# New TensorE prices in the build-time model that paces the background work of a two-block layer kernel

## The chip, the cores and the metric

The kernel runs on one core of one Trainium2 chip. The metric is device microseconds for one execution of the whole program, as the median of several runs.

## The reference, cut to what matters

256 tokens of width 2048 go through two blocks, one layer each. The first has latent attention beside differential attention, then cross-attention to a memory of 256 tokens, then a gated feed-forward layer of width 5632. The second has an adaptive norm, a wide input projection, a recurrent mix with matrix state (WKV) beside a short convolution, and an output projection. What the change touches most is where one block hands over to the other:

```python
x = x + (silu(hf @ w_gate) * (hf @ w_up)) @ w_down      # end of block 1
x = rms_norm(x, g_final)                                # its last norm
...
h = rms_norm_2(x, pre_gain) * (1.0 + scale) + shift     # block 2
proj = h @ w_in
pa = proj[..., :COLS_A]
pa = pa + (shift_time(pa, 1) - pa) * mu_shift           # token shift: row t takes in row t-1
r, k, v = pa[..., :D_A], pa[..., D_A:2*D_A], pa[..., 2*D_A:3*D_A]
...
S = S * w_t + sa * b_t + v_t * k_t                      # WKV, in chunks in the kernel
```

## The kernel before, in words

Every weight product is done in fp32r in three parts: the weight is split into a high and a low half (`whi`, `wlo`), the activation too, and TensorE (PE) adds `whi` with both halves of the activation and `wlo` with its high half. The weights come from memory in sub-tiles of 512 KB (two k tiles of 128 by 512 columns). For each sub-tile SP issues the load into `raw`, ScalarE (ACT) rounds it to `whi` (`act`, L401), VectorE (DVE) subtracts to get `wlo` (`tt`, L371), and PE runs twelve matmuls (`mm`, L410): eight with `whi`, then four with `wlo`. The rings hold 5 `raw`, 4 `whi` and 4 `wlo` buffers (L345), and `ahead` (L579) writes the splits of the next sub-tiles into the program before the matmuls of the present one. This is the main stream; it is a fixed sequence of sub-tiles over both blocks. The first two sub-tiles of block 2 are staged aside, in `own`.

All else is background work: generators that write a few instructions at each step (norms, transposes `tpose` L414 through the identity, attention, the token shift, the WKV chunks). Those that finish a column block are called posts, the long ones lanes. Nothing on the chip schedules them. The program's order is settled while it is built: after each eight and after each twelve matmuls of the main stream, `poll` (L495) asks a rough model of the engines, `Clock` (L241 to L324), whether a step's inputs will be there, and if so writes the step at that place into the queues of all the engines. The two conditions are that the step is due at least 900 ns before the model's PE time (`EARLY`), and, for lanes, that the modelled DVE and ACT are no more than 3000 ns ahead of PE (`SLACK`):

```python
EARLY, SLACK, ADA_BEAT = -900.0, 3000.0, 2
...
now = ck.t["PE"]
for g in posts + lanes:
    if not g.busy and g.due <= now + g.early and (g in posts or max(ck.t["V"], ck.t["S"]) <= ck.t["PE"] + SLACK):
        step(g)
```

Each engine then runs its own queue strictly in that order and waits where an input is late. So a price in the model moves no instruction from one engine to another; it moves background steps ahead of or behind main-stream instructions in the queues.

Three pieces of background work matter below. `ev_norm` (L1247) does the last norm of block 1 and the norm of block 2 for one half of the tokens, and writes the transposed halves `XA`, from which block 2's first matmuls read. `shift_mix` (L1287) does the token shift of a column block: it zeroes one row, copies the block one partition down by a DMA of GpSimd's (POOL's) queue, and then three DVE operations (subtract, scale, add) use what was copied; `ev_pa` (L1340) calls it for the 384 columns of `k` group 0 and for the 512 columns each of `r` and `v` later. `wkv_lane` (L1416) is the chain of the WKV mix, with `lora` (L1427) and the product with a triangle of ones (`mm` into `bgt`, L1472) at its start.

Of the kernel before, what the change touches and what calls it, by code (L numbers as in the profile page):

```python
# [11 lines left out]
F32R = mybir.dt.float32r  # L12
# [21 lines left out]
# block 2's input projection: the low rank columns lie before the key's  # L34
# [9 lines left out]
COLV = [("g_mix", 16), ("g_xattn", 16), ("g_mem", 16), ("g_ffn", 16), ("pre_gain_2", 16), ("post_gain_2", 16), ("ada_b_2", 48),  # L44
        ("g_q_lat", 4), ("g_kv_lat", 2), ("g_diff_sub", 2)]
# [46 lines left out]
def _kt(n):  # L92
    """k tiles to a transfer of n columns"""
    return 4 if n <= 256 else 2
# [51 lines left out]
class Arena:  # L146
    """Column ranges of one on-chip tile, handed out in program order."""
# [66 lines left out]
class Fixed(Buf):  # L214
    """A part of a tile that is not the arena's."""
# [8 lines left out]
class XT:  # L224
    """A transposed activation, split, 8 k tiles to a part: [128 channels, k, hi/lo, tokens]."""
# [18 lines left out]
class Clock:  # L244
    """A rough model of when each engine reaches what has been issued, to pace the background work."""
# [53 lines left out]
    def pe(self, cols, ins, outs):  # L299
        """the array's clock is halved after a window in which it was mostly idle"""  # L300
        w = int(max(self.t["PE"], self.after(ins, outs, "PE")) / 3413.3)
        self.op("PE", cols / (2.4 if self.cols.get(w - 1, 0) >= 3060 else 1.2) + 3, ins, outs)
        w = int(self.t["PE"] / 3413.3)
        self.cols[w] = self.cols.get(w, 0) + cols
# [18 lines left out]
class Job:  # L323
    """A column block's product: k tiles ka to kb of the weight with the activation's from k0 on.  # L324
    A skewed one runs through the first half of the tokens before the second; half is the
    evacuation of one half then."""
# [9 lines left out]
def kernel(ctx: ExitStack, tc: tile.TileContext, d, out):  # L336
    nc = tc.nc
    V, S, G, PE = nc.vector, nc.scalar, nc.gpsimd, nc.tensor
# [16 lines left out]
    A, A2 = Arena(big, NA - 352), Arena(big, 352, NA - 352)  # L355
# [8 lines left out]
    ck = Clock()  # L364
# [42 lines left out]
    def mm(o, l, r, start=True, stop=True):  # L407
        n = size(o)
        ck.pe(n if l.dtype == F32R else max(4 * n, 512) if l.shape[-1] > 64 else 2.3 * n, [l, r], [o])
        PE.matmul(out=o, lhsT=l, rhs=r, start=start, stop=stop, skip_group_check=True)  # L410

    def tpose(o, i):
        ck.pe(256, [i], [o])
        PE.transpose(o, i, ident)  # L414
# [39 lines left out]
    def rpow(o, a, scale, eps):  # L454
        """o = (a * scale + eps) ** -0.5 for a few columns"""
        ts(o, a, scale, eps, ALU.mult, ALU.add)
        gpow(o)
# [12 lines left out]
    # ------------------------------------------------------------------ engine  # L470
    class Task:
        """A generator, and when what its next step reads is there."""
# [44 lines left out]
    def run(jobs, hook):  # L517
# [6 lines left out]
        def early():  # L524
            """block 2's first weights, staged beside the ring"""
            yield from wait("own_go")
            xc = ck.slot(sb.tile([P, 4, 4, 256], F32R, tag="XC", name="own"), "XC", 1)
            at = [(xc[:, 0], xc[:, 1]), (xc[:, 2], xc[:, 3])]
            for i, (h, l) in zip(sorted(own), at):
                yield from room(1024)  # L530
                raw = buf(4, 256)
                dma(raw.ap, weight(i))
                yield [raw.ap]
                act(h, raw.ap, AF.Copy)
                yield
                tt(l, raw.ap, h.bitcast(F32), ALU.subtract)
                raw.free()
                his[i], los[i] = h, l
# [15 lines left out]
        def pieces(i):  # L554
            """the first one is cut, for an early start"""
            n = subs[i][0].kt
            return [slice(a, a + 1) for a in range(n)] if i == 0 else [slice(0, n)]
# [21 lines left out]
        def ahead(i):  # L579
            """what can be staged while sub-tile i is multiplied"""  # L580
            while True:
                for x in range(3):
                    while at[x] in own:
                        at[x] += 1
                nl, nh, nd = at
                if nl < nh and (nl < i + NL or nl < e0 + 4) and ringed(i, nl) < NL:
                    low(nl)
                    at[0] += 1
                elif nh < nd and (nh < i + NH or nh < e0 + 4) and ringed(i, nh) < NH:
                    high(nh)  # L590
                    at[1] += 1
                elif nd < len(subs) and ringed(nl, nd) < NR:
                    load(nd)
                    at[2] += 1
                else:
                    return
# [49 lines left out]
    # ------------------------------------------------------- transposes, splits  # L646
    def split_t(tr, xt, k, n, gain=None):
        """tr: [128, n, 256] in PSUM, transposed; into xt's k..k+n"""
        if gain is None:
            act(xt.hi(k, n), tr, AF.Copy)  # L650
            tt(xt.lo(k, n), tr, xt.hi(k, n).bitcast(F32), ALU.subtract)
        else:
            for a in range(n):
                hi, lo = xt.hi(k + a), xt.lo(k + a)
                src, gn = tr[:, a:a + 1, :], gain[:, a:a + 1]
                act(hi, src, AF.Copy, scale=gn)
                stt(lo, src, gn, hi.bitcast(F32), ALU.mult, ALU.subtract)
        xt.done(k, n)

    def trans(src, n=2):  # L660
        """natural [128 tokens, 2 halves, n*128] -> PSUM [128, n, 256]"""
        tr = pst("tr", 2).rearrange("p (a t) -> p a t", a=2)
        for a in range(n):
            for th in range(2):
                tpose(tr[:, a, th * P:th * P + P], src[:, th, a * P:a * P + P])
        return tr[:, 0:n, :]
# [8 lines left out]
    def to_t(src, dst, nk):  # L675
        """natural -> transposed fp32 [128, nk, 256]"""
        for a in range(0, nk, 2):
            tr = trans(src[:, :, a * P:(a + 2) * P])
            if a % 4 == 0:
                act(dst[:, a:a + 2, :], tr, AF.Copy)  # L680
            else:
                vcopy(dst[:, a:a + 2, :], tr)
            yield [src]
# [16 lines left out]
    def load_split(src, gain, xt, ahead):  # L700
        """a transposed activation from DRAM, with its gain, split"""
# [28 lines left out]
    # ================================================================ schedule  # L730
    with tc.manual_schedule():
# [28 lines left out]
        # ---- what block 1 keeps  # L760
# [5 lines left out]
        def tables():  # L766
# [32 lines left out]
            # lambda  # L799
# [13 lines left out]
            # tables that carry the norm's factor  # L813
# [17 lines left out]
        def xr_lane():  # L831
            """the residual stream, by column blocks of 512"""
# [8 lines left out]
        # ---- block 1, attention: evacuations  # L841
# [3 lines left out]
        def rope(o, p, cc, ss, n, hd):  # L845
            """o = p * cc + swap(p) * ss for [128, n heads * hd] (p in PSUM)"""
# [54 lines left out]
        def ev_scaled(key, k, nk, r, flag):  # L901
            """scaled by the norm's factor, then transposed"""
# [41 lines left out]
        # ---- attention lanes  # L944
        def softmax_head(score, scale, sums):
            """scores of one head -> exponentials and their sums"""
# [116 lines left out]
        # ---- residual updates  # L1063
        def ev_add(a, n, nxt=None):
            """xr += block; then, if asked for, its squares and its transpose with a gain"""
# [61 lines left out]
        # ---- FFN  # L1127
# [24 lines left out]
        # ---- adaLN vector, in the background of the FFN  # L1152
# [3 lines left out]
        def ada_lane():  # L1156
# [27 lines left out]
            # shift, gain and gate, then as rows  # L1184
# [25 lines left out]
        # ---- end of block 1: final norm, block 2's norm  # L1210
# [36 lines left out]
        def ev_norm(th, p):  # L1247
            """the two norms of a half of the tokens, their factors as one:
            (mean(x^2 g^2) + eps (mean(x^2) + eps)) ** -0.5"""
# [34 lines left out]
        # ================================================================ block 2  # L1284
        b2 = {}

        def shift_mix(raw, col, n):  # L1287
            """token-shift mix of a block [128, 2, n], in place"""
# [13 lines left out]
        def ev_lo(p):  # L1302
            """the low rank part, and the key's first 128 columns"""
# [108 lines left out]
        # ---- WKV  # L1412
# [3 lines left out]
        def wkv_lane(g):  # L1416
# [16 lines left out]
            # normalised key, key and beta  # L1433
# [20 lines left out]
            # decay: chunk factors, cumulated from both ends  # L1454
# [40 lines left out]
            # es: kk^, ep: r^, av: b^, kx: k^  (all natural)  # L1495
# [28 lines left out]
            # stacked operands of the state's update  # L1524
# [8 lines left out]
            # Gram blocks  # L1533
# [12 lines left out]
            # inverses of the 32 x 32 diagonal blocks, one per partition  # L1546
# [64 lines left out]
            # the chain over chunks  # L1611
# [45 lines left out]
            # group norm, bonus, gate  # L1657
# [29 lines left out]
        # ---- merge, output projection, gated residual  # L1687
# [80 lines left out]
        # ================================================================ the jobs  # L1768
# [64 lines left out]
        # ---- background work that starts when a weight is reached  # L1833
        def after(name, w, n=0):
            """a flag that is set when the n-th product with a weight is done"""
# [48 lines left out]
```

## Time and profile before

| | us |
|---|---|
| runs shown | 2036.32, 2033.89, 2034.57 |
| median | 2034.57 |
| profiled execution: span from the first to the last instruction | 2032.9 |
| its own time beside the span | not listed apart; the median lies 1.7 above the span |
| PE busy | 1997.7 |
| DVE busy | 1335.3 |
| ACT busy | 939.6 |
| POOL busy | 192.9 |
| mean granted clock of PE, as a share of full speed | 0.996 |

PE has work for 98% of the span. What it waited for, by engine, line and tile, is listed in the view of waits; the view of windows says in which stretch of the span that was.

### The profile page before, as it was taken

To read this page: it belongs to the slowest core of one execution; us is meant where nothing else is said; L and a number is where in the kernel's file an instruction comes from. 1 tells how busy PE (TensorE), PEld (TensorE's weight loads), DVE (VectorE), ACT (ScalarE), POOL (GpSimd) and SP (SyncE) were. 2 spreads that over 40 slices of the span, in tenths; PEclk is the share of its full clock that TensorE was granted. 3 is DMA by queue.
4 is the path that set the end of the run, shared out by engine and by line. 5 is a ranking of instruction groups with operands and counts; after the bars stand their busy time and mean duration, and the time that the engine had idled before them with its cause. 6 is when DMAs were issued, how large, how long until landed. Compare 5 with 4: busy or idle time off the path is not lost. (4 is left out here: it accounts for less than half of the span.)

```text
span 2032.9 us, 26782 instructions
## 1 busy us (share of the span) xinstructions
PE 1997.7 (98%) x10155; PEld 1663.1 (82%) x10155; DVE 1335.3 (66%) x1672; ACT 939.6 (46%) x1262; POOL 192.9 (9%) x316
## 2 busy tenths in 40 slices
PE   8999999999999999999999988899999999999998
PEld 7877888978888888888888886688888788888887
DVE  6756567456777767777754663768938678936654
ACT  6544458555444344434444453434444544444443
POOL 0000001000010100101000032120121201111000
PEclk9999999999999999999999999999999999999999
DMA  8643647547878888788776645676665666645763
GB/s 297 212 135 117 200 148 251 177 152 272 295 277 284 289 284 281 281 288 307 264 249 191 216 130 161 188 207 197 214 186 178 210 187 187 209 141 183 241 187 124
DMA packets 125056, 436.97 MB, mean 215 GB/s; under 512 B 17142, under 2 KB 17286, under 8 KB 124160
## 3 DMA queue, kind: packets, MB, share of 16 engines
q1 hardware_dynamic: 97776, 348.96, 52.0%
q0 software_dynamic: 26432, 85.19, 13.5%
q8 instruction: 79, 1.29, 0.2%
q10 hardware_dynamic: 720, 1.13, 0.2%
q14 instruction: 49, 0.40, 0.1%
HBM read 420.89 MB, written 5.79 MB: 210 GB/s over the span
## 5 line engine op out<-in xcount | busy, mean ns | idle before, releaser
L371 DVE TENSOR_TENSOR wlo<-raw,whi 128x1024 fp32r<-128x1024 f32 (+3 forms) x661 | 797.3, 1214 | 490.8 <-ACT whi L401 455.8
L401 ACT ACTIVATE whi<-raw 128x1024 fp32r<-128x1024 f32 (+3 forms) x661 | 689.9, 1051 | 627.8 <-PE mm L410 608.6
L410 PE MATMUL mm<-whi,XA 128*128 128x512 f32 (+3 forms) x3776 | 921.3, 385 | 7.3 <-ACT XA L401 5.5
L410 PEld LDWEIGHTS mm<-whi,XA 128*128 128x128 f32 x3776 | 689.3, 189 | 145.7 <-ACT XA L401 5.5
L410 PE MATMUL mm<-wlo,XA 128*128 128x512 f32 (+3 forms) x1888 | 495.0, 385 | 7.4 <-DVE wlo L371 7.4
L410 PEld LDWEIGHTS mm<-wlo,XA 128*128 128x128 f32 x1888 | 345.2, 189 | 77.2 <-DVE wlo L371 8.3
L410 PE MATMUL mm<-whi,XB 128*128 128x512 f32 (+1 forms) x1456 | 324.6, 366 | 0.1
L410 PEld LDWEIGHTS mm<-whi,XB 128*128 128x128 f32 x1456 | 249.9, 189 | 42.4 <-ACT whi L401 0.3
L383 DVE SCALAR_TENSOR_TENSOR arena<-arena 128x1024 f32<-128x1024 f32 (+24 forms) x180 | 180.8, 1005 | 1.5
L410 PE MATMUL mm<-wlo,XB 128*128 128x512 f32 (+1 forms) x728 | 174.3, 365 | 0.0
L410 PEld LDWEIGHTS mm<-wlo,XB 128*128 128x128 f32 x728 | 126.3, 189 | 21.7 <-DVE wlo L371 0.3
L371 DVE TENSOR_TENSOR arena<-arena 128x1024 f32<-128x1024 f32 (+8 forms) x101 | 91.7, 915 | 33.4 <-DMA arena<-arena 25.6
L430 POOL DMA_DIRECT2D arena<-in_ada_w_dram x96 | 50.7, 530 | 472.8 <-DVE arena L383 415.1
L410 PE MATMUL mm<-whi,XC 128*128 128x512 f32 (+1 forms) x368 | 87.3, 377 | 0.0
L401 ACT ACTIVATE arena<-arena 128x512 f32<-128x512 f32 (+5 forms) x84 | 51.3, 615 | 59.2 <-DVE arena L371 33.4
L410 PEld LDWEIGHTS mm<-whi,XC 128*128 128x128 f32 x368 | 64.2, 189 | 11.0
L414 PE MATMUL tr<-cst,arena 128*128 128x128 f32 x402 | 62.6, 274 | 4.6 <-DVE XA L371 3.4
L414 PEld LDWEIGHTS tr<-cst,arena 128*128 128x128 f32 x402 | 49.6, 141 | 17.5 <-DVE XA L371 3.7
L371 DVE TENSOR_TENSOR arena<-arena,mm 128x512 f32<-128x512 f32 (+1 forms) x74 | 44.9, 638 | 17.8 <-PE mm L410 14.4
L426 POOL TENSOR_TENSOR small<-small,cst 128x2 f32<-128x2 f32 (+1 forms) x16 | 11.4, 711 | 473.5 <-DVE small L378 405.8
L410 PE MATMUL bgs<-arena 128*128 128x256 f32 (+3 forms) x200 | 50.3, 360 | 0.0
L401 ACT ACTIVATE arena<-mm,small 128x512 f32<-128x512 f32 (+1 forms) x50 | 30.5, 660 | 35.9 <-PE mm L410 34.1
(126 smaller groups left out, 941.7 us busy)
## 6 DMA issues: line engine op xcount, KB each, us to landing
raw<-in_w_in_dram SPq DMA_DIRECT2D x241, 512.0 KB, 4.2
arena<-in_ada_w_dram POOLq DMA_DIRECT2D x96, 512.0 KB, 5.9
raw<-in_w_gate_dram SPq DMA_DIRECT2D x88, 512.0 KB, 5.0
raw<-in_w_up_dram SPq DMA_DIRECT2D x88, 512.0 KB, 5.0
raw<-in_w_down_dram SPq DMA_DIRECT2D x88, 512.0 KB, 4.6
raw<-in_w_out_dram SPq DMA_DIRECT2D x64, 512.0 KB, 3.6
raw<-in_p_b_dram SPq DMA_DIRECT2D x16, 512.0 KB, 3.5
raw<-in_p_a_dram SPq DMA_DIRECT2D x16, 512.0 KB, 4.5
```

The source lines that it names most:

```text
L371: V.tensor_tensor(out=o, in0=a, in1=b, op=op)
L383: V.scalar_tensor_tensor(out=o, in0=a, scalar=s, in1=b, op0=o0, op1=o1, **kw)
L401: S.activation(out=o, in_=i, func=f, scale=scale, **kw)
L410: PE.matmul(out=o, lhsT=l, rhs=r, start=start, stop=stop, skip_group_check=True)
L414: PE.transpose(o, i, ident)
L426: G.tensor_tensor(out=o, in0=o, in1=nhalf[:, 0:o.shape[1]], op=ALU.pow)
L430: (nc.sync if q == "SP" else nc.gpsimd).dma_start(out=o, in_=i)
```

## The change

The diff takes three prices of the model and replaces them. All its other lines remove comments.

```diff
@@ Clock.pe (L299)
-        self.op("PE", cols / (2.4 if self.cols.get(w - 1, 0) >= 3060 else 1.2) + 3, ins, outs)
+        self.op("PE", cols / (2.4 if self.cols.get(w - 1, 0) >= 3060 else 1.2), ins, outs)
@@ mm (L407)
         n = size(o)
-        ck.pe(n if l.dtype == F32R else max(4 * n, 512) if l.shape[-1] > 64 else 2.3 * n, [l, r], [o])
+        ck.pe(n + 32 if l.dtype == F32R else 4 * n + (224 if n >= 256 else 22), [l, r], [o])
@@ tpose (L412)
-        ck.pe(256, [i], [o])
+        ck.pe(240, [i], [o])
```

No instruction is added or removed: PE has 1105 background matmuls and transposes before and after, DVE 917 instructions of its background, ACT 494, and the order of SP's loads is the same. The places at which background work stands between main-stream instructions differ. Three of them follow, each as it was and as it is now.

PE where block 2 begins and the second half of the tokens is transposed, before (`tr` is a transpose into PSUM, `mm_9440` and `mm_9441` are the sums of the first and the second half of the tokens, `own` one of the two staged sub-tiles):

```order
L410 MATMUL mm_9440<-whi_9386,XA1_9404 128x256 x8
L410 MATMUL mm_9440<-wlo_9388,XA1_9404 128x256 x4
L414 MATMUL tr_9529<-cst_63,arena_66 128x128 x2
L410 MATMUL mm_9441<-own_7381,XA0_9403 128x256 x4
L414 MATMUL tr_9538<-cst_63,arena_66 128x128 x2
L410 MATMUL mm_9441<-own_7381,XA0_9403 128x256 x4
L414 MATMUL tr_9547<-cst_63,arena_66 128x128 x2
L410 MATMUL mm_9441<-own_7381,XA0_9403 128x256 x4
L414 MATMUL tr_9556<-cst_63,arena_66 128x128 x2
```
PE there, after:

```order
L410 MATMUL mm_9440<-whi_9386,XA1_9404 128x256 x8
L414 MATMUL tr_9525<-cst_63,arena_66 128x128 x2
L410 MATMUL mm_9440<-wlo_9388,XA1_9404 128x256 x4
L414 MATMUL tr_9534<-cst_63,arena_66 128x128 x2
L410 MATMUL mm_9441<-own_7381,XA0_9403 128x256 x8
L414 MATMUL tr_9547<-cst_63,arena_66 128x128 x2
L410 MATMUL mm_9441<-own_7381,XA0_9403 128x256 x4
L414 MATMUL tr_9556<-cst_63,arena_66 128x128 x2
```
The first two pairs of transposes stand one group of four matmuls earlier, and the transposes after them have eight matmuls of the second half of the tokens behind them where there were four.

DVE at the token shift of `k` group 0, before (each `wlo` is a sub-tile of the column block `r` group 0; `arena 128x256` and `128x2x128` are steps for the 128 columns that came with the low-rank part, `128x768` those for the 384 columns; the first of each is the one that reads the DMA's copy):

```order
L371 TENSOR_TENSOR wlo_9816<-raw_9711,whi_9814 128x1024
L371 TENSOR_TENSOR wlo_9836<-raw_9730,whi_9834 128x1024
L371 TENSOR_TENSOR arena_66<-arena_66 128x256
L371 TENSOR_TENSOR wlo_9859<-raw_9751,whi_9857 128x1024
L371 TENSOR_TENSOR arena_66<-arena_66 128x256
L371 TENSOR_TENSOR wlo_9878<-raw_9776,whi_9876 128x1024
L371 TENSOR_TENSOR arena_66<-arena_66 128x2x128
L371 TENSOR_TENSOR arena_66<-arena_66 128x768
L371 TENSOR_TENSOR wlo_9898<-raw_9798,whi_9896 128x1024
L371 TENSOR_TENSOR arena_66<-arena_66 128x768
L371 TENSOR_TENSOR wlo_9917<-raw_9818,whi_9915 128x1024
L371 TENSOR_TENSOR arena_66<-arena_66 128x2x384
```
DVE there, after:

```order
L371 TENSOR_TENSOR wlo_9816<-raw_9711,whi_9814 128x1024
L371 TENSOR_TENSOR arena_66<-arena_66 128x256
L371 TENSOR_TENSOR wlo_9837<-raw_9730,whi_9835 128x1024
L371 TENSOR_TENSOR wlo_9859<-raw_9751,whi_9857 128x1024
L371 TENSOR_TENSOR arena_66<-arena_66 128x256
L371 TENSOR_TENSOR arena_66<-arena_66 128x768
L371 TENSOR_TENSOR wlo_9879<-raw_9776,whi_9877 128x1024
L371 TENSOR_TENSOR arena_66<-arena_66 128x2x128
L371 TENSOR_TENSOR arena_66<-arena_66 128x768
L371 TENSOR_TENSOR wlo_9899<-raw_9798,whi_9897 128x1024
L371 TENSOR_TENSOR arena_66<-arena_66 128x2x384
```
The first `128x256` stands one `wlo` earlier, and so does the first `128x768`: three `wlo` lie between the two before, and two after. One `wlo` fewer is ahead of the first `128x768`.

PE at the first steps of the WKV chain in the column block after that, before (`bgs` and `bgt` are background sums; the eight of `128x2` and the `bgt` from `arena` and the constants are the triangle product and what goes with it):

```order
L410 MATMUL mm_9990<-whi_9984,XA0_9403 128x512 x4
L410 MATMUL mm_9991<-whi_9984,XA0_9403 128x512 x4
L410 MATMUL bgs_10068<-cst_63,arena_66 128x2 x8
L410 MATMUL mm_9990<-wlo_9986,XA0_9403 128x512 x2
L410 MATMUL mm_9991<-wlo_9986,XA0_9403 128x512 x2
L410 MATMUL mm_9990<-whi_10008,XA1_9404 128x512 x4
L410 MATMUL mm_9991<-whi_10008,XA1_9404 128x512 x4
L410 MATMUL bgt_10099<-arena_66,cst_63 128x512
```
PE there, after:

```order
L410 MATMUL mm_9990<-wlo_9966,XA0_9403 128x512 x2
L410 MATMUL mm_9991<-wlo_9966,XA0_9403 128x512 x2
L410 MATMUL bgs_10054<-cst_63,arena_66 128x2 x8
L410 MATMUL mm_9990<-whi_9984,XA0_9403 128x512 x4
L410 MATMUL mm_9991<-whi_9984,XA0_9403 128x512 x4
L410 MATMUL bgt_10081<-arena_66,cst_63 128x512
```
The row of eight stands ahead of that sub-tile's `whi` group and not behind it, and the triangle's matmul is one sub-tile earlier, behind the `whi` group of the fifth sub-tile and not of the sixth.

From there on the WKV chain keeps moving: counted in main-stream matmuls, its first transposes after that place stand 48 matmuls earlier (4 sub-tiles), and its last ones 156 earlier (13 sub-tiles).

## Rows read from the trace of the kernel before

**Rows 1.** The page: the span, and busy time of each engine.
```profile
span 2032.9 us, 26782 instructions
...
PE 1997.7 (98%) x10155; PEld 1663.1 (82%) x10155; DVE 1335.3 (66%) x1672; ACT 939.6 (46%) x1262; POOL 192.9 (9%) x316
```

**Rows 2.** Waits of PE, whole span: us in total, times, longest.
```profile
PE mm L410 <- DVE wlo L371: 7.4, 1, 7.4
PE mm L410 <- ACT XA L401: 6.8, 3, 5.5
PE bgt L410 <- DVE arena L383: 5.0, 1, 5.0
PE tr L414 <- DVE XA L371: 3.4, 1, 3.4
PE mm L410 <- ACT whi L401: 1.6, 1, 1.6
```

**Rows 3.** Windows: length, PE, PEld, DVE, ACT, POOL busy, PEclk, DMA share, GB/s.
```profile
0.00:100.00 100.00, 94.49 (x452) 80.20 (x453) 66.37 (x127) 64.70 (x103) 4.64 (x11) 1.00 0.73 254
...
1200.00:1300.00 100.00, 83.72 (x407) 68.71 (x405) 52.11 (x66) 42.07 (x67) 26.94 (x32) 0.95 0.55 164
...
1400.00:1500.00 100.00, 100.00 (x577) 82.25 (x576) 79.93 (x78) 45.57 (x49) 18.07 (x33) 1.00 0.69 214
```

**Rows 4.** Windows of 5 us at the hand-over, the same columns.
```profile
1195.00:1200.00 5.00, 5.00 (x33) 5.00 (x31) 2.08 (x6) 1.93 (x6) 0.00 (x0) 0.66 0.32 84
...
1255.00:1260.00 5.00, 0.90 (x4) 0.40 (x3) 0.00 (x0) 0.00 (x0) 0.00 (x0) 1.00 0.06 26
1260.00:1265.00 5.00, 1.69 (x4) 1.40 (x5) 3.83 (x4) 0.00 (x0) 0.00 (x0) 0.52 0.18 22
```

**Rows 5.** Timeline of PE, 1241 to 1300: start, length, operation, [idle before <-releaser].
```profile
1245.84 1.07 PE L410 MATMUL mm<-wlo,XA 128*128 128x512 f32 x4
...
1248.56 1.02 PE L410 MATMUL bgt<-arena 65*128 65x512 f32 x2
1249.42 1.02 PE L410 MATMUL bgs<-arena 65*128 65x512 f32 x2
...
1253.93 1.98 PE L410 MATMUL mm<-whi,XA 128*128 128x512 f32 x8
1263.31 2.07 PE L410 MATMUL mm<-wlo,XA 128*128 128x512 f32 x4 [7.41 <-DVE wlo L371]
...
1294.38 2.08 PE L410 MATMUL bgt<-arena,cst 128*128 128x512 f32 x2 [5.00 <-DVE arena L383]
```

**Rows 6.** Timeline of PE, 1196 to 1217.
```profile
1203.17 0.65 PE L410 MATMUL mm<-wlo,XA 128*128 128x256 f32 x4
...
1204.89 0.38 PE L410 MATMUL mm<-own,XA 128*128 128x256 f32 x1 [0.85 <-ACT XA L401]
1205.86 0.62 PE L410 MATMUL mm<-own,XA 128*128 128x256 f32 x3 [0.59 <-DVE XA L371]
...
1207.18 1.08 PE L410 MATMUL mm<-own,XA 128*128 128x256 f32 x4 [0.47 <-ACT XA L401]
...
1208.95 1.78 PE L410 MATMUL mm<-own,XA 128*128 128x256 f32 x8
```

**Rows 7.** Timeline of DVE, at the norm and at the two shifts.
```profile
1202.86 2.61 DVE L383 SCALAR_TENSOR_TENSOR arena<-arena,small 128x256 f32<-128x256 f32 x4 [0.66 <-POOL small L426]
...
1243.78 0.43 DVE L371 TENSOR_TENSOR arena<-arena 128x256 f32<-128x256 f32 x1 [6.30 <-DMA arena<-arena]
...
1261.17 0.96 DVE L371 TENSOR_TENSOR arena<-arena 128x768 f32<-128x768 f32 x1 [14.02 <-DMA arena<-arena]
...
1288.64 1.23 DVE L371 TENSOR_TENSOR arena<-arena 128x1024 f32<-128x1024 f32 x1 [5.27 <-DMA arena<-arena]
```

**Rows 8.** DMA issues, 1180 to 1310, then 1270 to 1900: KB each, median us to landing.
```profile
arena<-arena POOLq DMA_DIRECT2D x1, 381.0 KB, 26.7
...
arena<-arena POOLq DMA_DIRECT2D x7, 508.0 KB, 5.5
```

## The prediction

> **What bounds the kernel now.** I read the page first: PE is busy for 1997.7 of a span of 2032.9 us, and no other engine for more than two thirds of it [rows 1]. So a change that only reorders can win back at most what PE waits for, plus what it loses at its lower clock. The view of waits gives the first: five rows with 24.2 us together, of which 5.5 (inside the 6.8) is the wait for the first input at the start [rows 2]. The windows of 100 us say where the rest lies: between 1200 and 1300 us PE is busy for 83.72 of 100 us and its clock falls to 0.95; from 1400 to 1500, with DVE at its busiest (79.93), PE is busy for the full 100 [rows 3]. The hand-over from block 1 to block 2 is thus the one stretch in which anything is to be won, apart from the start; everywhere else a reordering can only leave the time or add a wait.
>
> In the hand-over the 5-us windows show the lower of the two clock levels (1.2 instead of 2.4 GHz): 0.66 in 1195 to 1200 and 0.52 in 1260 to 1265, after PE had been idle for 4.1 of the 5 us before [rows 4]. The timeline of PE puts the two large waits at 1263.31 (7.41 us, for a `wlo`) and 1294.38 (5.00 us, for the DVE operation that frees `bgt`) [rows 5], and that of DVE says what is behind both: DVE stood at an operation of the token shift for 14.02 us, and for 5.27 us later, until a DMA had landed [rows 7]. DVE's queue is in order, so a `wlo` behind such an operation waits with it. The DMA is the copy of `k` group 0's 384 columns, 26.7 us from issue to landing [rows 8]; while it ran alone it moved 26 GB/s at a share of 0.06, about one of sixteen DMA engines [rows 4].
>
> **What the change does to the model.** For the main stream's matmul of 512 columns the model charged 512 / 2.4 + 3 = 216.3 ns, and now (512 + 32) / 2.4 = 226.7. From 1245.84, where four of them start, to 1248.56, with the next eight between, twelve take 2.72 us [rows 5], which is 226.7 ns each: the new price is the trace's. The Trainium skill, "TensorE: Matmul & The Clock Gate", Part 1, section "Wait — 56ns, not 53.3ns?", gives 215.7 ns for back-to-back matmuls of 512 columns at the higher clock; by that the old price would be right and the new one 5% dear. The trace disagrees, with 226.7. For fp32 at 512 columns the model goes from 856 to 947 ns, where two in a row start 0.86 us apart [rows 5]; those prices get worse, but they are few.
>
> So the modelled PE runs about 4.8% later against DVE, ACT, POOL and the DMAs, whose prices stay. A step falls due after fewer main-stream matmuls, and the limit on DVE and ACT opens sooner: background work goes into the queues earlier or at the same place, never later by much. No instruction is added or removed, so PE's 1997.7 us of work stay except where the clock differs. The cost lies in who waits for whom, at three places.
>
> **1. Norm of the second token half.** PE waited 0.85, 0.59 and 0.47 us for the halves of the first transposes, 1.91 in all [rows 6]. Now the first pair stands before the four matmuls that began at 1203.17 and not behind them, 0.5 us earlier, and the second pair stands ahead of the `own` matmuls that had come between. On DVE the norm's own steps stand ahead of two operations of 128x256 on the other half's transposes, some 0.43 us each as such a one takes, so the scaling that began at 1202.86 [rows 7] begins some 0.85 us earlier. The eight `own` matmuls then need the low half of the first pair at about 1205.0 rather than 1205.86, and the second pair's is there; they end near 1206.1 where they ended at 1208.1. Gain 2.0 us. At the least nothing, if ACT, which makes the high halves, is as late as before; at the most 3.0, if the 8-matmul group at 1208.95, which took 1.78 us, tightens too. The 3.4-us wait for the first half [rows 2] has the same order around it and stays.
>
> **2. Token shift of `k` group 0.** DVE meets the first operation on the 384 columns one `wlo` earlier. PE therefore runs dry one sub-tile (2.72 us) earlier: at the four matmuls that began at 1253.0, 0.9 us before the eight at 1253.93, instead of at 1255.9 (1263.31 less 7.41) [rows 5]. If the copy landed when it did, PE would resume at the same moment with 2.72 us less done. But one `wlo` fewer frees one `raw` buffer fewer, so one 512-KB load fewer shares the DMA engine; its sixteenth is 32 KB, which at 26 GB/s [rows 4] takes 1.26 us there. I take the landing as 1.3 us earlier: +1.4 net. Bounds: 0, if two loads' worth is saved, and +3.5, if nothing is and some 0.8 us of half clock comes on top. A gain is left to the rivals. The 128-column shift ahead of it also moves one `wlo` up: DVE waits there until 1243.78 [rows 7], and that `wlo`, behind the 0.43 of the operation and with 1.23 for its own 128x1024 as in [rows 7], would be ready near 1245.4; PE asks at 1245.84 [rows 5]. It fits by 0.4 us; this is the thinnest place.
>
> **3. Start of the WKV chain.** The triangle's matmuls stand one sub-tile earlier, but what they wait for comes down to the shift of `r`, whose copy DVE awaited until 1288.64 [rows 7]. That copy is issued behind the same DVE work after the first stall, so it lands with it. The wait of 5.0 us begins a sub-tile earlier and ends some 1.3 us earlier: the loss of place 2 is carried on, not doubled. 0.
>
> **The rest.** From 1300 on the chain's steps come 4 to 13 sub-tiles earlier. PE has no wait there to lose. `wlo` runs up to four sub-tiles ahead, 10.9 us, and at 79.93% [rows 3] DVE has the time. Some transposes now stand closer behind what they read: like the 0.47 to 0.85 us of [rows 6], one such wait here or there. I take +0.5; bounds 0 and +4 (five or six of them).
>
> **Sum.** −2.0 + 1.4 + 0 + 0.5 = −0.1 us on a span of 2032.9. The median of the runs is 2034.57, 1.7 above it, and I carry that over: 2034.5. The bounds added up run from −3 to +7.5; all of one sign together is unlikely, so the likeliest case has 2031 to 2038.
>
> **The rivals.**
>
> *Slower: a second copy holds DVE.* What turned the shift into a PE wait was that DVE stood longer than the ring could cover: it stopped at 1247.15 (1261.17 less 14.02) and PE ran dry at 1255.9, so 8.8 us is the point from which a hold costs. Where the later `r`, `v` and `k` group 1 shifts are met sooner after their copies' issue, one could pass it. For it: 128-column holds of 6.30 are already near [rows 7], and one copy took 26.7 us. Against it: the seven later 508-KB copies took 5.5 us in the median [rows 8]. The price is that of the known one, 7.4 us plus 1 to 2 at half clock: 2034.5 + 9 = about 2043.
>
> *Faster: the shift's copy lands early.* If with a load or two fewer beside it the copy lands 5 us sooner, the first wait shrinks to some 3 us and the half clock behind it goes: with 4 to 5 us from there, 2 of half clock, and the norm, some −7: 2027.5. For it: 381 KB in 26.7 us [rows 8] are 15 GB/s, so for a good part of its time it had less than the 26 GB/s. Against it: 26 GB/s was all that it reached alone [rows 4].
>
> *Slower: the new price is too dear.* If the array's matmul were really the old 216.3 ns, background work would be queued 5% too soon everywhere, and transposes and small fp32 products would stand ahead of their inputs, at 0.5 to 0.9 us each [rows 6]; ten of them make +7, 2041. Twelve matmuls in 2.72 us [rows 5] speak against it. It is what the rule of the Trainium skill's page named above would make of this change.
>
> *Nothing is moved where it matters* gives 2034.6, and lies inside the likeliest case.
>
> **Numbers.** 0.2%, 4.1 us here, is about what a measurement of this kernel tells from no change: the same is 2030.5 to 2038.6. The likeliest case has 0.57, nearly all of it inside. The second hold has 0.17, the dear price 0.04 and the shift that gains nothing back with waits on top 0.02, all slower; the early landing has 0.20, faster. Rounded: faster 0.21, the same 0.56, slower 0.23. The range leaves out the outer half of either side case: 2028.5 to 2042.5.
>
> **What would show it.** Place 1: the first `own` matmul of the second half waits 0.4 us or less, and the 0.59 and 0.47 are gone. Place 2: one wait of 8.5 to 9.5 us for a `wlo`, one sub-tile earlier, in place of 7.41; the 384-column copy takes 25 us or so. Place 3: a `bgt` wait near 5 us, one sub-tile earlier. After 1300: PE at 100 of 100 in each window. The prediction is wrong if the copy's time changes by several us, if a wait for `wlo` appears behind the 128-column shift or any shift after 1300, or if PE's busy time changes beyond the clock's part.

## The result, and the profile after

The changed kernel takes 2048.65 us (median of 4 runs, 2044.89 to 2049.67) against 2034.24 for the one before: a ratio of 1.0063, 95% interval 1.005 to 1.0077. It is slower by about 13 us, outside the range that was given (2028.5 to 2042.5). The profiled execution has a span of 2047.3 us against 2032.9 [rows 1]: 14.4 to account for.

The page of the changed kernel, span and busy times:

```profile
span 2047.3 us, 26801 instructions
...
PE 2004.5 (98%) x10155; PEld 1666.3 (81%) x10155; DVE 1336.2 (65%) x1672; ACT 939.9 (46%) x1262; POOL 191.7 (9%) x316
```

The page counts 19 instructions more, none of them among the busy ones: their numbers are the same on every engine. PE is busy for 6.8 us more on the same work. The granted clock accounts for most of it: summed over windows of 5 us, leaving out the idle end, it cost 4 to 7 us more than before, depending on how much of each low stretch was busy. The other 7.6 us are idle. The waits of PE, whole span (total, times, longest), to be held against [rows 2]:

```profile
PE mm L410 <- DVE wlo L371: 10.2, 4, 8.8
PE tr L414 <- DVE arena L371: 6.3, 6, 2.5
...
PE bgt L410 <- DVE arena L383: 5.3, 1, 5.3
PE tr L414 <- DVE XA L371: 3.8, 2, 3.5
```

The wait for `wlo` has grown from 7.4 to 10.2, and the wait of transposes for DVE, 1.1 us in three before (0.5 at the most), is now 6.3 in six (2.5 at the most). The windows say where (length; PE, PEld, DVE, ACT, POOL busy; PEclk; DMA share; GB/s), with the row of 100 to 200 before ahead of them:

```profile
100.00:200.00 100.00, 99.48 (x452) 75.16 (x451) 57.31 (x98) 46.73 (x87) 0.76 (x1) 1.00 0.41 130
```

```profile
100.00:200.00 100.00, 97.67 (x436) 73.60 (x435) 55.11 (x94) 45.79 (x85) 2.91 (x4) 0.98 0.38 118
...
1200.00:1300.00 100.00, 82.21 (x411) 69.18 (x412) 51.78 (x70) 40.25 (x68) 27.04 (x32) 0.92 0.53 160
...
1400.00:1500.00 100.00, 96.47 (x625) 78.15 (x624) 68.22 (x64) 41.02 (x46) 16.97 (x31) 0.98 0.59 186
```

The hand-over is worse (82.21 busy and 0.92, against 83.72 and 0.95 in [rows 3]); but 100 to 200 and 1400 to 1500, where PE had lost nothing or half a microsecond, now lose 2.3 and 3.5 each and drop to 0.98 of the clock. In windows of 5 us, where the clock fell:

```profile
115.00:120.00 5.00, 3.75 (x13) 3.22 (x14) 2.34 (x5) 1.54 (x2) 0.00 (x0) 0.66 0.35 105
...
1265.00:1270.00 5.00, 2.43 (x6) 1.95 (x7) 4.58 (x6) 0.00 (x0) 0.00 (x0) 0.50 0.21 70
...
1300.00:1305.00 5.00, 5.00 (x13) 3.41 (x12) 2.96 (x3) 3.06 (x5) 0.51 (x1) 0.59 0.46 136
1430.00:1435.00 5.00, 2.49 (x11) 1.85 (x10) 4.96 (x5) 1.65 (x2) 0.00 (x0) 0.88 0.51 159
1435.00:1440.00 5.00, 5.00 (x20) 4.06 (x20) 4.97 (x6) 2.86 (x5) 0.00 (x0) 0.78 0.68 210
```

**The hand-over**, place by place. Four rows of PE's timeline before, then its timeline now:

```profile
1189.88 1.19 PE L410 MATMUL mm<-whi,XB 128*128 128x256 f32 x8
1194.53 0.44 PE L414 MATMUL tr<-cst,arena 128*128 128x128 f32 x2 [3.45 <-DVE XA L371]
...
1215.99 1.55 PE L410 MATMUL mm<-whi,XA 128*128 128x384 f32 x8
...
1295.47 3.50 PE L410 MATMUL mm<-whi,XA 128*128 128x512 f32 x8
```

```profile
1196.71 1.20 PE L410 MATMUL mm<-whi,XB 128*128 128x256 f32 x8
1201.35 0.44 PE L414 MATMUL tr<-cst,arena 128*128 128x128 f32 x2 [3.45 <-DVE XA L371]
...
1212.10 1.10 PE L410 MATMUL mm<-own,XA 128*128 128x256 f32 x7 [0.35 <-DVE XA L371]
...
1220.92 1.55 PE L410 MATMUL mm<-whi,XA 128*128 128x384 f32 x8
...
1251.28 1.20 PE L410 MATMUL mm<-wlo,XA 128*128 128x512 f32 x4 [0.33 <-DVE wlo L371]
...
1267.57 2.08 PE L410 MATMUL mm<-wlo,XA 128*128 128x512 f32 x4 [8.83 <-DVE wlo L371]
...
1299.24 2.08 PE L410 MATMUL bgt<-arena,cst 128*128 128x512 f32 x2 [5.32 <-DVE arena L383]
1300.33 4.17 PE L410 MATMUL mm<-whi,XA 128*128 128x512 f32 x8
```

From the transposes that end the 3.45-us wait to the first matmul of 384 columns (1215.99 before, 1220.92 now) it took 21.46 us before and takes 19.57 now. Of the waits of 0.85, 0.59 and 0.47 [rows 6] one of 0.35 is left in the second half, and one of 0.32 is new ahead of it (1207.88). From the group of four at 1203.17 [rows 6], which begins at 1210.65 now, 2.55 us are won; the first half, ahead of that group, takes 0.66 longer. From that matmul to the group of eight behind the second large wait (1295.47 before, 1300.33 now) lie 79.48 and 79.41 us, but one sub-tile less has been done, 2.72 us; and this group takes 4.17 us where it took 3.50. DVE shows why, as in [rows 7]:

```profile
1249.66 0.43 DVE L371 TENSOR_TENSOR arena<-arena 128x256 f32<-128x256 f32 x1 [8.68 <-DMA arena<-arena]
...
1265.42 0.96 DVE L371 TENSOR_TENSOR arena<-arena 128x768 f32<-128x768 f32 x1 [12.73 <-DMA arena<-arena]
...
1293.49 1.23 DVE L371 TENSOR_TENSOR arena<-arena 128x1024 f32<-128x1024 f32 x1 [5.52 <-DMA arena<-arena]
```

It waits for the copy once more, with one `wlo` fewer done ahead of that wait. (Between the first `128x256` and the first `128x768` two `wlo` stand before as well as after, not three and two; both operations have moved up by one.) The copy took 26.0 us (26.7 in [rows 8]), and PE's wait for `wlo` is 8.83 instead of 7.41. A small wait for `wlo` is new at 1251.28, behind the 128-column shift that DVE left at 1249.66.

**Block 1.** The last eight matmuls ahead of the 3.45-us wait begin at 1196.71, and at 1189.88 before: 6.8 us are lost by then. The largest piece is at 111 to 118 us. The first transposes of a rope output before, then PE there now, and the DVE operation that counts:

```profile
116.49 0.55 PE L414 MATMUL tr<-cst,arena 128*128 128x128 f32 x3 [0.52 <-DVE arena L371]
```

```profile
110.92 1.98 PE L410 MATMUL mm<-whi,XC 128*128 128x512 f32 x8
112.73 1.07 PE L410 MATMUL mm<-wlo,XC 128*128 128x512 f32 x4
113.64 0.27 PE L414 MATMUL tr<-cst,arena 128*128 128x128 f32 x1
116.25 0.90 PE L414 MATMUL tr<-cst,arena 128*128 128x128 f32 x3 [2.33 <-DVE arena L371]
116.80 2.06 PE L410 MATMUL mm<-whi,XC 128*128 128x512 f32 x4
```

```profile
114.12 1.35 DVE L371 TENSOR_TENSOR arena<-mm,arena 128x512 f32<-128x512 f32 x3
```

These transposes stand eight matmuls earlier than they did, three of them wait 2.33 us for DVE, and the clock falls behind the wait (0.66 above). The rest is lost between 270 and 360 us, counted along the main stream: from 272 to 460 PE has eight waits of 0.27 to 0.64 us, 2.8 together, where it had three of 0.27 to 0.33 before.

**The WKV chain.** PE, then DVE, at 1420 to 1438:

```profile
1422.58 1.20 PE L410 MATMUL mm<-wlo,XA 128*128 128x512 f32 x4 [0.62 <-DVE wlo L371]
...
1425.98 1.20 PE L410 MATMUL mm<-wlo,XA 128*128 128x512 f32 x4 [0.38 <-DVE wlo L371]
...
1433.34 0.73 PE L414 MATMUL tr<-cst,arena 128*128 128x128 f32 x4 [2.51 <-DVE arena L371]
```

```profile
1429.68 1.21 DVE L371 TENSOR_TENSOR wlo<-raw,whi 128x1024 fp32r<-128x1024 f32 x1
1430.82 2.47 DVE L371 TENSOR_TENSOR arena<-arena 128x1024 f32<-128x1024 f32 x2
1433.20 2.35 DVE L371 TENSOR_TENSOR wlo<-raw,whi 128x1024 fp32r<-128x1024 f32 x2
1435.47 1.74 DVE L383 SCALAR_TENSOR_TENSOR arena<-arena 64x900 f32<-64x900 f32 x1
1437.25 1.08 DVE L405 TENSOR_REDUCE arena<-arena 64x30 f32<-64x900 f32 x1
```

DVE runs without a gap, and its queue is behind: `wlo` comes late twice (0.62, 0.38), and the transposes at 1433.34 wait 2.51 us for the operations at 1430.82. What is left of the difference behind the hand-over is 14.4 − 6.8 + 1.9 − 3.3 = 6.2 us: 3.5 of these waits; the rest was not taken apart, and the lower clock (0.88 and 0.78 above) is part of it.

### The profile page after: what moved, and what is told of

Its sections match the earlier page's. It is cut to its first block, busy times and chain, and to the rows that moved or that the text cites. A ratio compares the mean times of both kernels' runs of the same rounds, so it can differ in the third digit from the quotient of the medians.

```text
span 2047.3 us, 26801 instructions
## 1 busy us (share of the span) xinstructions
PE 2004.5 (98%) x10155; PEld 1666.3 (81%) x10155; DVE 1336.2 (65%) x1672; ACT 939.9 (46%) x1262; POOL 191.7 (9%) x316
## 4 chain that ended last, share of the span: by engine, by line
PE 89%; DVE 4%; issue 2%; ACT 2%; DMA 2%; POOL 1%; DVEq 0%; POOLq 0%; ACTq 0%; SPq 0%
PE mm L410 81%; PE bgs L410 3%; PE tr L414 2%; PE bgt L410 2%; DMA arena<-arena 2%; DVE wlo L371 1%; DVE arena L371 1%; ACT arena L401 1%; DVE arena L383 1%; ACT whi L401 1%; POOL arena L430 0%; ACT XA L401 0%; PE tr L410 0%; DMA arena<-in_xt_dram 0%; PE bgt L414 0%
## 5 line engine op out<-in xcount | busy, mean ns | idle before, releaser
L410 PE MATMUL mm<-wlo,XA 128*128 128x512 f32 (+3 forms) x1888 | 495.8, 385 | 10.2 <-DVE wlo L371 10.2
```

## The experiments

Times are medians, with the ratio to the kernel before, timed beside it, and its 95% interval; the kernel before stood at 2035.5 to 2035.8 in these runs, so ratios compare better than times.

**Which price.** One run takes only the main stream's price, one only the others:

```diff
# a1_main                                       # a2_small
+ if l.dtype == F32R: ck.pe(n + 32, ...)        + if l.dtype == F32R: ck.pe(n, ..., 3.0)
+ else: ck.pe(<old>, ..., 3.0)                  + else: ck.pe(<new>, ...)   # and 240 for transposes
```

> Only the price of the main stream's fp32r matmul is new (n + 32); the fp32 and transpose prices are those of before. Theory A, that the later PE clock of the model puts background steps ahead of their inputs at three places (first transposes of block 1 near 113 us, the hand-over, the WKV chain near 1430 us), expects nearly all of the loss: 2044 to 2050 us, with a PE wait for DVE of over 2 us near 113 us. Rival B, that the fp32 and transpose prices, which the trace does not bear out (947 against 860 ns), do it, expects 2034 to 2037.

> Only the fp32 and transpose prices are new; the fp32r matmul keeps 216.3 ns. Theory A expects little: 2033 to 2039, and no PE wait over 1 us outside the hand-over. Rival B expects the whole loss, 2044 to 2050.

Measured: 2047.97, 1.0061 (1.0049 to 1.0074), and 2028.96, 0.9964 (0.9951 to 0.9976). The main stream's price makes the whole loss, with waits for DVE of 2.33 us near 113 and 3.26 at 1428. The other prices by themselves make a gain, which neither theory had; it does not show when both are new. PE's two large waits in the second run, for `wlo` and for `bgt`, are 6.2 and 2.0 us, 1.2 and 3.0 shorter than before: the same two waits, met at other moments.

**Which stage.** The new prices up to the down projection of block 1 only, and from there on only:

```diff
+ if j.w == "w_down": ck.new = False     # a3_block1; a4_later starts False and turns True
```

> All new prices, but only up to the down projection of block 1; the old ones from there on. Theory A, with places that add up by themselves, expects the first place alone: 2034.2 + 6 to 7, so 2040 to 2041.5, with the waits of before at the hand-over (7.4 and 5.0). A rival C, that the places are not independent because every later wait hangs on where the earlier ones put the clock and the DMAs, expects a time that is off this by 3 or more.

> The old prices up to the down projection of block 1, and the new ones from there on. Theory A expects the hand-over and the WKV chain alone: 2034.2 + 7 to 8, so 2041 to 2042.5, with a wlo wait of about 8.8 at the hand-over and the waits of 0.6 and 2.5 near 1420 to 1430. Rival C expects a time that is off this by 3 or more.

Measured: 2040.04, 1.0018 (1.0009 to 1.0027), and 2041.03, 1.0026 (1.0016 to 1.0036): +4.5 and +5.5 in medians, 10 together against the 13 of the whole. Each loss is some 2 us below what theory A expected (6 to 7, and 7 to 8), and the sum is 3 below the whole; the intervals allow that the places add up, but don't show it closely. The waits are those that A expected: 7.1 and 4.5 at the hand-over in the first, and 8.5 there with 0.65, 0.37 and 2.53 in the WKV chain in the second. In the first one's profile (of its fastest run, 2036.39) the wait of 2.33 near 113 us is there, but the clock did not fall behind it.

**The WKV chain.** The model charges the inverse's products, which read one operand transposed, 68 + 1.04 ns an element like any other (the 130 in the expectation should read 68): 1.00 us for 900 elements. At 1435.47 above one takes 1.78 us to the next operation.

```diff
+ ck.t["V"] += 115 + 0.8 * i * i
  stt(tv, N[q, 0:i, 0:i].rearrange("p j c -> p c j"), -1.0, ...
```

> The changed kernel, with one more price put right: the product with a transposed read in the triangular inverse, which the model charges 130 + 1.04 ns an element and the trace shows at 1.80 us for 900 elements against 1.00, gets 115 + 0.8 ns an element on top. Theory A (in the WKV chain DVE is overbooked because these products are priced too low, and the old low PE price had hidden that) expects the waits of 0.6, 0.4 and 2.5 us near 1420 to 1433 and the half clock behind them to go: 4 to 5 us less than the changed kernel, 2042.5 to 2045. Rival D, that these waits come from a late weight load there, expects them to stay, 2047 to 2050.

Measured: 2043.79, 1.0036 (1.0022 to 1.005), as theory A expected. No PE wait of 0.2 us or more is left after 1310 us, and PE is busy for the full 100 from 1400 to 1500:

```profile
1400.00:1500.00 100.00, 100.00 (x616) 82.46 (x615) 71.65 (x67) 43.89 (x48) 16.99 (x31) 1.00 0.69 203
```

**The transposes near 113 us.** Written out while building, the kernel's model has PE waiting 3.8 us there for a DVE operation that reads a PSUM buffer of the main stream: it takes the four buffers to rotate by count. In the trace there is no such wait: the rows at 110.92 and 112.73 run through, while DVE does the reading at 114.12 to 115.47. So the model's PE time jumps ahead of the chip's, and the transposes fall due too early.

```diff
  for ap in outs:
      k, a, b = self.span(ap)
+     if e == "PE" and k[0] == "mm": continue
```

> The changed kernel, but in the model PE no longer waits for the readers of the main stream's PSUM buffers. The model has such a wait of 3.8 us near 110 us, and the trace has none there: PE runs through, and meets the transposes too early. Only a handful of PE rows near 113 us move (the first transposes stand behind twelve more matmuls). Theory A expects the 2.3-us wait there to fall below 0.6 and the half clock behind it to go: 2 to 4 us less than the changed kernel, 2044.5 to 2046.5. Rival E, that the model's wait is true and only the place of the step's DVE work matters, expects no change, 2048 to 2050.

Measured: 2043.83, 1.0039 (1.0027 to 1.0052). The transposes stand sixteen matmuls later and nothing waits:

```profile
116.09 1.07 PE L412 MATMUL mm<-whi,XC 128*128 128x512 f32 x4
117.01 0.60 PE L416 MATMUL tr<-cst,arena 128*128 128x128 f32 x4
```

The first edit is inside what was expected, the second 0.7 us below it; twelve matmuls had been expected in place of sixteen. Their gains, 0.27% and 0.24% of the time, 5 us each, are known to 3 us.

**The copy, by its price.** The model prices POOL's copies at 180 GB/s. The copy of the shift gets 14.6:

```diff
- dma(sh[1:P, :, :], raw[0:P - 1])
+ dma(sh[1:P, :, :], raw[0:P - 1], rate=14.6)   # end = go + 2650 + size / rate
```

> The changed kernel, with the copy of the token shift priced at 14.6 GB/s (381 KB in 26.7 us, as the trace of before shows) in place of 180. Its steps come later then, and DVE doesn't stand at them with wlo behind it. Theory A expects the wait of 8.8 at the hand-over to fall below 1, that of 5.3 too or to half, and the half clock behind them to go: 14 to 18 us less than the changed kernel, 2031 to 2035. Rival F, that the copy is then slowed by the loads that go on beside it and something later waits for it instead, expects less than 6 us, 2043 or more.

> The kernel before, with that price of the copy alone. Theory A expects 10 to 15 us less than before, 2020 to 2025: the waits of 7.4 and 5.0 go, with 4 us of half clock. Rival F expects less than 5 us, 2030 or more.

Measured: 2034.39, 0.9992 (0.9984 to 1.0001), and 2027.85, 0.9962 (0.9949 to 0.9974). The first is as theory A expected in time; the second lies 3 us above what A expected and below rival F's. In mechanism A is half right: the wait for `bgt` goes, but one for `wlo` stays, 9.3 and 9.5 us, later on. DVE's wait and the DMA issues of 1235 to 1248 (KB, us to landing) in the second:

```profile
1273.23 0.42 DVE L371 TENSOR_TENSOR arena<-arena 128x256 f32<-128x256 f32 x1 [17.89 <-DMA arena<-arena]
```

```profile
arena<-arena POOLq DMA_DIRECT2D x1, 381.0 KB, 33.1
arena<-in_rowv_dram POOLq DMA_DIRECT2D x1, 256.0 KB, 26.9
arena<-arena POOLq DMA_DIRECT2D x1, 127.0 KB, 30.5
```

With the loads going on beside it the copy takes 33.1 us, and what POOL issued after it, even a load of a row vector from memory, takes 27 to 30. The copy of 127 KB, at 14.6 GB/s some 12 us in the model, lands late because of the one ahead of it. A price that looks at each copy by itself does not mend that.

**The copy, by its shape.** The 127 rows go as 112 and 15:

```diff
- dma(sh[1:P, :, :], raw[0:P - 1])
+ dma(sh[1:113, :, :], raw[0:112])
+ dma(sh[113:P, :, :], raw[112:P - 1])
```

> The kernel before, with the copy of the token shift in two, 112 rows and 15, in place of 127; prices as before. Theory G, that the strided 127-row copy runs on one DMA engine (26 GB/s alone, 15 beside the loads) and holds up all that is queued behind it, expects the 381 KB to land in under 12 us, the wlo wait of 7.4 to fall below 1 and that of 5.0 to half or less: 2034.2 less 9 to 14, 2020 to 2026. Rival F, that POOL's copies are starved by the weight loads whatever their shape, expects copies of 20 us or more and 2030 or more.

> The changed kernel with the same split. Theory G expects the waits of 8.8 and 5.3 to go the same way: 2048.6 less 12 to 18, 2031 to 2037; the losses near 113 and 1430 us stay, so it stays 8 to 11 above the split kernel of before. Rival F expects 2043 or more.

Measured: 2016.22, 0.9907 (0.9892 to 0.9922), and 2029.21, 0.9966 (0.9954 to 0.9979). Both waits of the hand-over are gone. The first time is 4 us below the best that was expected, the second 2 below; the second is 13 above the first, where 8 to 11 was expected. The first one's copies, and its window there:

```profile
arena<-arena POOLq DMA_DIRECT2D x1, 336.0 KB, 8.1
...
arena<-arena POOLq DMA_DIRECT2D x1, 45.0 KB, 8.0
```

```profile
1200.00:1300.00 100.00, 97.85 (x480) 82.62 (x479) 67.09 (x78) 51.30 (x74) 24.73 (x39) 0.98 0.66 205
```

Rival F falls. The gap between the new prices and the old is 13 us with the split too. So the hand-over, on which the prediction spent most of its words, is no part of what the change costs once the copy is quick: PE is busy for 97.77 of that window with the new prices, and for 97.85 with the old.

**All three edits**, with the new prices and the old:

> The changed kernel with the split copy, the true price of the inverse's products, and without the PSUM wait that the model has and the chip has not. If the three places are all there is to the loss, 2048.6 less 15, less 5, less 5: 2022 to 2026, with PE waits of 2 us in all outside the start and the first norm half. If other places take over (rival C), 2028 or more.

> The kernel before, its old PE prices, with the same three edits. It tells whether the right PE price is worth anything once the model's other errors are out. If the old price helped only by offsetting those errors, this is not faster than the changed kernel with the three: 2021 to 2028, and the two within 3 us of each other. If the old price is the better by itself, it is 4 us or more ahead.

Measured: 2019.65, 0.9922 (0.9908 to 0.9936), and 2015.60, 0.9905 (0.9891 to 0.9918). The gap falls from 13 us to 4, and the intervals overlap a little. The two edits of the model do it: on top of the split they are worth 9.6 us with the new prices (2029.21 to 2019.65), and 0.6 with the old (2016.22 to 2015.60). The old PE price had hidden both errors. Of the two conditions on record, within 3 us or 4 and more, the 4.05 meets the second by a hair. The profiles say where it lies: the wait ahead of the first norm half ends at 1197.32 with the new prices and at 1193.65 with the old, so 3.7 of the 4.0 us between the two spans are lost in block 1. Both times are below what was expected (2022 to 2026, and 2021 to 2028), since the split was worth more; the old prices with the three are the fastest kernel here, not told apart from the old prices with the split alone. What PE still waits for with the new prices and the three edits, beside the start and the first norm half, is about 5 us, where 2 had been expected; its largest rows:

```profile
PE tr L416 <- DVE arena L373: 1.8, 5, 0.6
PE bgt L416 <- DVE arena L373: 0.8, 1, 0.8
```

**The rest, by the margin**, and the small prices again:

```diff
- EARLY, SLACK, ADA_BEAT = -900.0, 3000.0, 2
+ EARLY, SLACK, ADA_BEAT = -1800.0, 3000.0, 2
```

> The changed kernel with the three edits, and with 1800 ns in place of 900 between a step's due time and the model's PE clock. Theory H, that the low PE price had served as a margin, a few per cent of the time since the step's inputs, and that a right price needs the margin in another place, expects the waits of 0.3 to 0.6 us between 250 and 460 us to go: 2015 to 2018, level with the old prices and the three edits. Rival I, that the margin has nothing to do with them, expects 2019 to 2022.

> The changed kernel with that margin alone. Theory H expects the small waits of block 1 to go, and perhaps the 2.3 us near 113, but not the hand-over (a copy of 26 us) and hardly the WKV chain: 2040 to 2046. If the margin is all that the change lost (rival J), it is back at 2033 to 2037.

> The new prices of fp32 and transposes with the old one of the main stream, and the three edits. Those prices alone had made 2029.0, mostly by shorter waits of 6.2 and 2.0 at the hand-over. If that was the copy's landing again, nothing of it is left here: 2014 to 2018, level with the old prices and the three. If these prices are worth something by themselves, 2008 to 2012.

Measured: 2036.66, 1.0006 (0.9997 to 1.0015); 2039.52, 1.0019 (1.001 to 1.0028); and 2020.18, 0.9925 (0.9911 to 0.9938). The larger margin does opposite things in the first two. With the three edits it costs 17 us (2019.65 to 2036.66). Alone, on the changed kernel, it wins back 9 of the 13 us (1.0063 to 1.0019), a little more than theory H expected; rival J is out.

In both the loss of block 1 is gone, though three waits of 0.4 us are left between 270 and 300 us: the wait ahead of the first norm half ends at 1193.40 and 1194.77 (1193.65 with the old prices and the three edits, 1194.53 before). In the second (its profile is of its slowest run, 2042.51) the waits of 1420 to 1434 are gone too, without the price of the inverse's products. What is lost comes near the end, where the WKV chain is late now and the transposes that feed the next product wait for it, at 1890 in the first and 1896 in the second:

```profile
PE tr L416 <- DVE arena L373: 15.2, 1, 15.2
```

```profile
PE tr L414 <- DVE arena L371: 5.8, 1, 5.8
```

So H was right about the cause in block 1, and the WKV chain gained as well, which it had not expected; it did not have what a late end of that chain costs. The small prices alone, with the three edits, are 2 us above the higher of the two ranges: their gain had been in the two waits at the copy, and in their run a wait of 3.3 us appears at the chain's late end.

## Why the prediction was wrong

**The norm half**: −2.0 forecast, −1.9 measured. The mechanism is the one given: two of the three waits are gone and the third is 0.35. That the number fits so closely is partly luck: 2.55 us were won in the second half, and 0.66 lost in the first.

**The shift of `k`**: +1.4 forecast, with 0 to 3.5; about +3.3 measured with what follows it (2.72 for the sub-tile not done, 0.7 more at the lower clock). The one longer wait, one sub-tile earlier, was within what was named (8.5 to 9.5). The term was too small because of the copy's 1.3 us only 0.7 were saved: 26.7 became 26.0, and DVE's wait ended at 44.5 us behind the first 384-column matmul instead of 45.2. At the second wait nothing was left of it. The place that was called the thinnest did not hold: the wait for `wlo` at 1251.28, 0.33 us, is one of the signs that were named for being wrong, and cost little.

**The start of the WKV chain**: 0 forecast, a wait near 5 us a sub-tile earlier; 5.3 measured. Right in that the loss is carried on and not doubled; the wait ended 0.07 us earlier and not 1.3, which is counted in the term above.

**The rest**: this step failed. It said +0.5, with 0 to 4, on the ground that "PE has no wait there to lose" and that DVE, at 79.93%, "has the time". It measured about 13, and PE was not at 100 of 100 in each window after 1300 (96.47 in 1400 to 1500), as had been named for a sign. Three things were wrong in it. The bound took each new wait as one of those seen, 0.47 to 0.85 us, and left out the clock behind it; two waits of 2.33 and 2.51 came with a drop of the clock. The busy share of a window of 100 us says nothing of 20 us in which products that take 1.8 us were priced at 1.0. And block 1, where 6.8 of the 13 were lost, was not in the sum at all: that transposes there move up to three sub-tiles could be read in the order, and how close the inputs were could be read in the trace.

The rival "the new price is too dear" had 0.04 and 2041. Its effect, steps queued ahead of their inputs, is what happened. Its cause is not: 226.7 ns is what the matmul takes. Steps came too early because a right PE price was set against a DVE price that is too low and a PSUM wait that isn't there, which a PE price that was too low had made up for. With those two put right the loss is 4 us, not 13, with the quick copy in both kernels; the 4 are in block 1, and a larger margin takes them away there. Which further prices make them is open.

**The clock** was carried as 0 to 0.8 us in one place. PE's busy time grew by 6.8 of the 14.4, and most of that is the clock.

The rival of the copy that lands early did not come about: the copy landed 0.7 us earlier, not 5. It put −7 on a part of the first wait; with both waits gone, by the split, 19 us are won on the kernel before.

## What to carry to other kernels

A build-time model that sets the order is tuned as a whole: a price that is put right can cost more than it gains as long as the others lean on it. Before one is changed, set the model's times for each engine against a trace and look where the order rests on the largest differences; here that was one DVE product, one wait and one copy. Where a queue waits for a transfer, the transfer's shape is to be looked at before the order: 112 and 15 rows in place of 127 were worth 19 us, more than any price, and as much with the new prices as with the old.

Background work can be late as well as early: a larger margin took away the waits at its inputs, worth 9 us on the changed kernel, and brought one of 6 to 15 us at its end.

## What the hardware showed

A copy on chip of 127 rows by 2 by 384, strided, took 26 to 33 us, at 24 to 26 GB/s when alone; 112 of its rows took 8.1 us, and a whole block of 127 rows of 4 KB 7.9. The Trainium skill, "DMA: Bandwidth & Descriptors", section "Why a DMA increments its semaphore by 16 and not by 1", says that a transfer is spread over the largest number of engines up to 16 that divides the outermost dimension of both its sides, one for 127, with some direct copies of POOL's queue as exceptions. The share of 0.06 [rows 4] and the three times agree with that. What POOL issued behind such a copy landed with it: a load of 256 KB took 26.9 us there, where five of that size took 5.2 in the median in the kernel before.

PE's waits cost nearly twice their idle time: 6.8 us of busy time, most of it the lower clock, beside 7.6 of idle. The drop does not follow each wait. Behind the same wait of 2.33 us near 113 us the granted clock of 115 to 120 us was 0.66 in the changed kernel and with the split and 0.70 with the copy's price, but 1.00 with the main stream's price alone, with the new prices in block 1 alone and with the inverse's price.
